# Low parts of weights issued later in the gate-matrix loop, and a pick's gelu and gate moved on ScalarE

## The chip, the core and the metric

The kernel runs on one core of one Trainium2 chip. The core has TensorE (PE, matrix products into PSUM; its weight loads are a row of their own, PEld), VectorE (DVE), ScalarE (ACT), GpSimd (POOL) and the queue of SyncE (SP), from which most DMAs are issued. Each engine works through its own list of instructions in order and waits for the others by semaphores. The metric is the device time of one execution in microseconds (us), the median of several runs.

## What is computed

A transformer-like layer over 512 latent tokens of width 1024: attention and a gating branch, and then a retrieval layer ("PEER"), which is the part that the change touches. Each token picks, for each of 8 heads, 16 out of 16384 experts; an expert is a row `u` and a row `v`, and the token's output is the sum of `gelu(x . u) * gate * v` over its 128 picks.

```python
def peer(h, w_query, sub_keys, u_tab, v_tab):
    ...
    best, pos = lax.top_k(cand, PEER_TOPK)
    eidx = jnp.take_along_axis(cidx, pos, axis=-1)
    gate = jax.nn.softmax(best, axis=-1)
    def one(args):
        xb, ib, gb = args
        act = jax.nn.gelu(jnp.einsum('td,thkd->thk', xb, u_tab[ib]), approximate=False) * gb.astype(xb.dtype)
        return jnp.einsum('thk,thkd->td', act, v_tab[ib])
```

## The kernel before

The 512 tokens are four tiles of 128. Three of them (`NB` = 3, 384 tokens) go the dense way: for each of 128 blocks of 128 experts TensorE computes all products with `u` (a **u pass**, `u_pass`, 24 matmuls into `ps_u`), ScalarE takes the gelu (`gS`), DVE multiplies by a dense matrix of gates (`Gc`, zero where an expert was not picked), and TensorE multiplies by `v` (a **v pass**, `v_pass`, 18 matmuls into `po`). The fourth tile goes by gathers: for each of its 128 picks POOL fetches the rows `u` and `v` (`fetch`, an indirect DMA into `uv`), DVE takes the **dot** with the token (`dot`, a product of 1024 with a running sum, line 846), the gelu and the gate follow, and DVE adds `v` times that to `acc` (`accumulate`, line 855). `gather_step` starts one fetch and takes the dot of the pick fetched three steps ago; `gather_end` finishes the picks in the list `pend`; `gather_to(share)` takes steps until a share of the picks is done.

All products are in three matmuls (`mm3`) of values split into a high and a low part. For each weight tile a DMA on SP's queue loads `w_raw` (four buffers), ScalarE rounds it to the **high part** `w_hi` (line 173), and DVE subtracts to get the **low part** `w_lo` (line 184, function `w_low`). `w_get` asks for the tiles of a pass and starts loads and splits of later ones. `hold[0]` decides when low parts are issued: if it is false, at once behind the high part; if it is true, they wait in `lows` until somebody calls `w_low`.

The dense gates are made in the **gate-matrix loop**, 48 turns (`batches`) of 8 tokens each. A turn i issues, in this order: `one_hots_b` of turn i+1 (8 instructions of DVE, `oh_b`), `gate_matrix` (16 matmuls of TensorE into `ps_G` from `oh_b` and `oh_a`, and two copies of ScalarE to `stg`), one u pass (with its gelu on ScalarE, and with the split of a weight tile for a later one), `one_hots_a` of turn i+2 (8 squares and a Relu of ScalarE, `oh_a`), some 2.8 us of top-16 and merge work for another token tile while there is any (`advance`), `gather_end`, and from turn 10 to turn 41 `gather_to`, 0.8 steps a turn. There are two buffers of `oh_b` and three of `oh_a`.

Behind it comes the **value stage**, 128 turns: a v pass each, from turn 74 on a u pass too up to turn 124, `a_hi` (DVE's `at`, ScalarE's `ah`), `a_lo` (DVE's `al`), and picks at the end of a turn. The lists of PE, DVE, ACT and POOL stand in the order in which this code is written (`manual_schedule`); the order of SP's queue is set by the scheduler.

Of the kernel before, what the change touches and what calls it, by code (L numbers as in the profile page):

```python
# [18 lines left out]
AF = mybir.ActivationFunctionType  # L19
ALU = mybir.AluOpType  # L20
# [38 lines left out]
def body(ctx, nc, tc, a, out):  # L59
# [91 lines left out]
    lows, hold = deque(), [False]  # L151
# [27 lines left out]
    def w_low(upto=None):  # L179

        while lows and (upto is None or lows[0][0] <= upto):
            i, lo, r, hi = lows.popleft()
            eng = nc.gpsimd if order[i] in on_pool else nc.vector
            eng.tensor_tensor(lo, r, hi.bitcast(F32), op=ALU.subtract)  # L184
# [385 lines left out]
    with tc.tile_pool(name="sg1", bufs=1) as s1, tc.tile_pool(name="sg2", bufs=2) as s2:  # L570
# [6 lines left out]
        with tc.tile_pool(name="pz", bufs=1, space=PSUM) as pzp, tc.tile_pool(name="pu", bufs=2, space=PSUM) as pu:  # L577
# [100 lines left out]
            for n in range(8):  # L678
                g = gate(0, n, gs_d)
# [152 lines left out]
    G_FROM = 10  # L832
    steps = [(t, k) for t in range(NB, NT) for k in range(P)]
    n_steps = len(steps)
    coming, pend = [], []

    def fetch(t, k):
        g = ge.tile([P, 2 * D], F32, name="uv", bufs=LEAD + 2)
# [4 lines left out]
    def dot(t, k, g):  # L843
        act = sm.tile([P, 1], F32, name="act")
        junk = ge.tile([P, D], BF16, name="dj")
        nc.vector.scalar_tensor_tensor(junk, g[:, :D], 1.0, h2A[t - NB], op0=ALU.mult, op1=ALU.mult, accum_out=act)  # L846
        return t, k, g, act

    def accumulate(t, k, g, act):
        nc.scalar.activation(act, act, AF.Gelu)  # L850
        nc.vector.tensor_tensor(act, act, gate[:, t, k:k + 1], op=ALU.mult)
        if k == 0:
            nc.vector.tensor_scalar_mul(acc[t - NB], g[:, D:], act)
        else:
            nc.vector.scalar_tensor_tensor(acc[t - NB], g[:, D:], act, acc[t - NB], op0=ALU.mult, op1=ALU.add)  # L855

    def gather_end(left=0):
        while len(pend) > left:
            accumulate(*pend.pop(0))

    def gather_step():
        gather_end(1)
        if len(coming) == LEAD or (coming and not steps):
            pend.append(dot(*coming.pop(0)))
        if steps:
            coming.append(fetch(*steps.pop(0)))

    def gather_to(share):
        while steps and n_steps - len(steps) < n_steps * share:
            gather_step()  # L870

    gS = {}
    with tc.tile_pool(name="k1", bufs=1, side="right") as k1:
# [104 lines left out]
        def advance(us):  # L978

            while us > 0 and any(todo):  # L980
                q = todo[0] or todo[1]
                d = next(q[0], None)
                if d is None:
                    q.popleft()
                else:
                    us -= d
            return any(todo)
# [74 lines left out]
        with tc.tile_pool(name="pg", bufs=3, space=PSUM) as pgp, tc.tile_pool(name="k2", bufs=2, side="right") as k2:  # L1062
            stg = {}

            pks, oas, obs = {}, {}, {}

            def picks_of(t):

                while t not in pks:
                    while t not in done:  # L1070
                        advance(1.0)
                    ef = efs.pop(t)
                    pt = pgp.tile([P, 3, P], F32, name="ps_pk", bufs=1)
                    for k in range(2):
                        nc.tensor.transpose(pt[:, k], ef[:, k].rearrange("p h k -> p (h k)"), ident)
                    nc.tensor.transpose(pt[:, 2], gate[:, t], ident)
                    pks[t] = k2.tile([P, 3, P], F32, name="pk")
                    nc.scalar.activation(pks[t], pt, AF.Copy)
                return pks[t]

            def one_hots_a(t, o):

                pk = picks_of(t)
                oa = oas[t, o] = k2.tile([P, 8, P], F32, name="oh_a", bufs=3)
                for i in range(8):
                    k = o * 8 + i
                    nc.scalar.activation(oa[:, i], iota, AF.Square, scale=-1.0, bias=pk[:, 1, k:k + 1])  # L1087
                nc.scalar.activation(oa, oa, AF.Relu, scale=-1.0, bias=ones[:, 0:1])

            def one_hots_b(t, o):  # L1090

                t0 = o * 8
                pk = picks_of(t)
                ob = obs[t, o] = k2.tile([P, 8, P], F32, name="oh_b")
                for i in range(8):
                    nc.vector.tensor_scalar(ob[:, i], iota, pk[:, 0, t0 + i:t0 + i + 1], pk[:, 2, t0 + i:t0 + i + 1],  # L1096
                                            op0=ALU.is_equal, op1=ALU.mult)

            def gate_matrix(t, o):

                oa, ob = oas.pop((t, o)), obs.pop((t, o))
                if o % 2 == 0:
                    stg[0] = k2.tile([P, NBLK // GCH, 16, GCH], F32, name="stg")
                for q in range(2):
                    pG = pgp.tile([P, 4, P], F32, name="ps_G")
                    for i in range(4):
                        nc.tensor.matmul(pG[:, i], oa[:, q * 4 + i], ob[:, q * 4 + i], start=True, stop=True)  # L1107
                    tt = o % 2 * 8 + q * 4
                    nc.scalar.activation(stg[0][:, :, tt:tt + 4].rearrange("p c t g -> p t c g"),
                                         pG.rearrange("p t (c g) -> p t c g", g=GCH), AF.Copy)  # L1110
                if o % 2:
                    tt = t * P + o // 2 * 16
                    nc.sync.dma_start(G_d[:, :, tt:tt + 16].rearrange("c p t g -> p c (t g)"),
                                      stg[0].rearrange("p c t g -> p c (t g)"))

            batches = [(t, o) for t in range(NB) for o in range(16)]
            while 0 not in done:
                advance(4.0)
                next_u()
            for _ in range(UA):  # L1120
                next_u()
            one_hots_a(*batches[0])
            for _ in range(UB):
                next_u()
            one_hots_a(*batches[1])
            one_hots_b(*batches[0])
            for i, (t, o) in enumerate(batches):
                if i + 1 < len(batches):
                    one_hots_b(*batches[i + 1])
                gate_matrix(t, o)  # L1130
                if nu[0] < n_ahead - RESERVE:
                    next_u()
                if i + 2 < len(batches):
                    one_hots_a(*batches[i + 2])
                advance(2.8)
                gather_end()
                if i >= G_FROM:
                    gather_to(PICKS_G * (i + 1 - G_FROM) / (G_TO - G_FROM) if i < G_TO else 0)
            advance(1000.0)
            while nu[0] < n_ahead:  # L1140
                next_u()


    with tc.tile_pool(name="e1", bufs=2, side="right") as e1, \
# [53 lines left out]
        for b in range(NBLK):  # L1198
            if b == 0:
                gelu_back(0)  # L1200
                gelu_back(1)
                g_load(0)
                parts = a_lo(*a_hi(0))
            if b + 2 < NBLK:
                gelu_back(b + 2)
            u_w = None
            if b >= SPILL and b + AHEAD < NBLK:
                u_w = w_get("u", b + AHEAD)
            else:
                v_w = w_get("v", b)  # L1210
            ah, al = parts
            nxt = None
            if b + 1 < NBLK:
                if (b + 1) % GCH == 0:
                    g_load((b + 1) // GCH)
                nxt = a_hi(b + 1)
            w_low()
            if nxt is not None:
                parts = a_lo(*nxt)
            if u_w is not None:  # L1220
                gS[b + AHEAD] = u_pass(b + AHEAD, u_w)
                v_w = w_get("v", b)
            if b == NBLK // 2:
                nc.sync.dma_start(gg2, rows_d[3:4].to_broadcast([P, D]))
            if b < NBLK - TAIL:
                v_pass(b, *v_w, ah, al, range(NB))
            else:
                tail.append((b, *v_w, ah, al))
            gather_end()
            if b < SPILL:  # L1230
                gather_to(PICKS_G + PICKS_V * (b - 3) / (SPILL - 4))
            else:
                gather_to(PICKS_G + PICKS_V + (1 - PICKS_G - PICKS_V) * (b + 1 - SPILL) / (NBLK - SPILL - 7))
            if not steps and coming:
                gather_step()
            w_low()
            if b == NBLK - 2:
                while coming:
                    gather_step()
                gather_end()  # L1240
                xn = [x_back(t) for t in range(NT)]
                for t in range(NB, NT):
                    finish(t, acc[t - NB], xn[t])
# [79 lines left out]
```

## Time and profile before

| | us |
|---|---|
| median of 3 runs | 2053.46 (2052.76 to 2057.22) |
| the profiled execution, its own time | 2056.82 |
| its span, from first to last instruction | 2055.1 |
| busy PE, DVE, ACT, POOL | 1934.7 (94%), 1610.0 (78%), 1007.2 (49%), 387.9 (19%) |

Times of day in the rows are us from the span's start. The rows of the trace give start, length, engine, line and what was written from what; a bracket at the end of a row holds the idle time of the engine before it and what ended that. A granted clock of 1.00 is TensorE's upper level (2.4 GHz), 0.50 its lower (1.2 GHz). The gate-matrix loop lies between 945 and 1270 us, the value stage from 1289 us on. An instruction's row is longer than the time after which its engine starts the next one, since they overlap at their ends.

### The profile page before, as it was taken

The numbers are of one execution on the slowest core, as the hardware profiler recorded it, in microseconds if no ns is written. First come the engines' busy times: TensorE is split into PE (matmuls) and PEld (weight loads), VectorE is DVE, ScalarE is ACT, GpSimd is POOL, SyncE is SP. The second block draws the span as 40 slices with busy tenths as digits, with TensorE's granted clock in tenths as the row PEclk, the third lists the DMA queues.
The fourth block names the chain that finished last, engine by engine and source line by source line (L and its number), as shares of the span: only waits on it lengthen the run. The fifth ranks groups of instructions, "written<-read, shape, count | busy, mean of one in ns | idle before, by whom it ended". The sixth has DMA issues, their size and how long they took to land.

```text
span 2055.1 us, 28329 instructions
## 1 busy us (share of the span) xinstructions
PE 1934.7 (94%) x10042; PEld 1697.7 (83%) x10042; DVE 1610.0 (78%) x3108; ACT 1007.2 (49%) x1947; POOL 387.9 (19%) x237
## 2 busy tenths in 40 slices
PE   6889999999999899888899999999999999999997
PEld 5767888887878798788889999788888899998996
DVE  7667777747755657999998785688888799898887
ACT  4335555535433355447888987333333333333333
POOL 0023232101000124330001110011111233333321
PEclk9999999999989999999999999999999999999999
DMA  8843323256755354445569998889899799989982
GB/s 320 281 159 91 89 82 96 84 193 217 236 166 199 128 160 151 135 169 203 179 194 322 309 324 284 301 315 338 326 335 321 269 343 356 341 322 340 346 314 96
DMA packets 171229, 484.40 MB, mean 236 GB/s; under 512 B 14384, under 2 KB 82896, under 8 KB 152528
## 3 DMA queue, kind: packets, MB, share of 16 engines
q1 hardware_dynamic: 152656, 348.37, 50.6%
q0 software_dynamic: 18432, 134.23, 17.9%
q8 instruction: 79, 1.29, 0.2%
q14 instruction: 62, 0.51, 0.1%
HBM read 424.72 MB, written 49.43 MB: 231 GB/s over the span
## 4 chain that ended last, share of the span: by engine, by line
PE 64%; DVE 15%; issue 6%; ACT 4%; DMA 2%; POOL 1%; SPq 0%; ACTq 0%; POOLq 0%; DVEq 0%
PE po L202 8%; PE po L203 8%; PE po L204 8%; PE ps_u L204 5%; PE ps_u L203 5%; PE ps_u L202 5%; PE ps_G L1107 2%; DVE w_lo L184 2%; PE ps_proj L202 2%; PE ps_proj L203 2%; PE ps_proj L204 2%; PE ps_s L488 2%; PE ps_o L522 2%; ACT oh_a L1087 1%; DVE oh_b L1096 1%
## 5 line engine op out<-in xcount | busy, mean ns | idle before, releaser
L173 ACT ACTIVATE w_hi<-w_raw 128x1024 fp32r<-128x1024 f32 x370 | 391.0, 1057 | 469.2 <-issue 263.3
L184 DVE TENSOR_TENSOR w_lo<-w_raw,w_hi 128x1024 fp32r<-128x1024 f32 x330 | 404.9, 1228 | 150.8 <-ACT w_hi L173 150.4
L839 POOL DMA_INDIRECT uv<-in_uv,eidx x128 | 208.7, 1631 | 876.9 <-DVE acc L855 537.5
L204 PE MATMUL ps_u<-h2B,w_lo 128*128 128x384 f32 x1024 | 348.3, 340 | 16.4 <-DVE w_lo L184 16.4
L202 PE MATMUL ps_u<-h2B,w_hi 128*128 128x384 f32 x1024 | 352.2, 344 | 1.1 <-ACT h2B L771 1.1
L203 PE MATMUL ps_u<-h2B,w_hi 128*128 128x384 f32 x1024 | 347.0, 339 | 0.6 <-DVE r L84 0.6
L202 PE MATMUL po<-w_hi,ah 128*128 128x512 f32 x768 | 304.5, 396 | 7.8 <-ACT ah L1180 7.8
L203 PE MATMUL po<-w_lo,ah 128*128 128x512 f32 x768 | 304.3, 396 | 0.9 <-DVE w_lo L184 0.9
L204 PE MATMUL po<-w_hi,al 128*128 128x512 f32 x768 | 304.2, 396 | 0.0
L204 PEld LDWEIGHTS ps_u<-h2B,w_lo 128*128 128x128 f32 x1024 | 194.3, 190 | 19.3 <-DVE w_lo L184 19.3
L202 PEld LDWEIGHTS ps_u<-h2B,w_hi 128*128 128x128 f32 x1024 | 194.9, 190 | 4.1 <-ACT h2B L771 1.4
L203 PEld LDWEIGHTS ps_u<-h2B,w_hi 128*128 128x128 f32 x1024 | 194.6, 190 | 3.8 <-DVE r L84 1.0
L202 PEld LDWEIGHTS po<-w_hi,ah 128*128 128x128 f32 x768 | 144.7, 188 | 41.0 <-ACT ah L1180 8.1
L204 PEld LDWEIGHTS po<-w_hi,al 128*128 128x128 f32 x768 | 144.7, 188 | 35.1
L203 PEld LDWEIGHTS po<-w_lo,ah 128*128 128x128 f32 x768 | 144.7, 188 | 34.1 <-DVE w_lo L184 1.3
L855 DVE SCALAR_TENSOR_TENSOR acc<-uv,act,acc 128x1024 f32<-128x1024 f32 x127 | 163.2, 1285 | 4.5
L846 DVE SCALAR_TENSOR_TENSOR dj<-uv,h2A 128x1024 bf16<-128x1024 f32 x128 | 156.2, 1220 | 0.9
L184 POOL TENSOR_TENSOR w_lo<-w_raw,w_hi 128x1024 fp32r<-128x1024 f32 x40 | 98.0, 2452 | 248.2 <-ACT w_hi L173 245.1
L1178 DVE TENSOR_TENSOR at<-gS,Gc 128x384 f32<-128x384 f32 x128 | 121.1, 946 | 9.1 <-DMA gS<-gS_d 9.0
L1180 ACT ACTIVATE ah<-at 128x384 fp32r<-128x384 f32 x128 | 66.2, 518 | 122.1 <-DVE at L1178 121.8
L813 ACT ACTIVATE gS<-ps_u 128x384 f32<-128x384 f32 x128 | 62.8, 491 | 128.7 <-PE ps_u L204 128.3
L1107 PE MATMUL ps_G<-oh_b,oh_a 128*128 128x128 f32 x768 | 100.7, 284 | 24.8 <-DVE oh_b L1096 24.3
(308 smaller groups left out, 3503.3 us busy)
## 6 DMA issues: line engine op xcount, KB each, us to landing
w_raw<-in_uT SPq DMA_DIRECT2D x128, 512.0 KB, 5.6
w_raw<-in_uv SPq DMA_DIRECT2D x128, 512.0 KB, 6.3
w_raw<-in_w SPq DMA_DIRECT2D x120, 512.0 KB, 3.8
G_d<-stg SPq DMA_DIRECT2D x24, 1024.0 KB, 5.8
Gc<-G_d SPq DMA_DIRECT2D x16, 1536.0 KB, 10.1
ada_w<-in_wada SPq DMA_DIRECT2D x32, 512.0 KB, 10.0
w_raw<-in_wada SPq DMA_DIRECT2D x32, 512.0 KB, 4.3
gS_d<-gS SPq DMA_DIRECT2D x74, 192.0 KB, 4.0
```

Source lines behind the costliest of these rows:

```text
L173: nc.scalar.activation(hi, r, AF.Copy)
L184: eng.tensor_tensor(lo, r, hi.bitcast(F32), op=ALU.subtract)
L202: nc.tensor.matmul(ps, lh, rh, start=first, stop=False)
L203: nc.tensor.matmul(ps, lh, rl, start=False, stop=False)
L204: nc.tensor.matmul(ps, ll, rh, start=False, stop=last)
L813: nc.scalar.activation(g, ps, AF.Gelu)
L839: nc.gpsimd.indirect_dma_start(out=g, out_offset=None, in_=a["uv"], in_offset=bass.IndirectOffsetOnAxis(ap=eidx[:, t - NB, k:k + 1], axis=0))
L846: nc.vector.scalar_tensor_tensor(junk, g[:, :D], 1.0, h2A[t - NB], op0=ALU.mult, op1=ALU.mult, accum_out=act)
L855: nc.vector.scalar_tensor_tensor(acc[t - NB], g[:, D:], act, acc[t - NB], op0=ALU.mult, op1=ALU.add)
L1107: nc.tensor.matmul(pG[:, i], oa[:, q * 4 + i], ob[:, q * 4 + i], start=True, stop=True)
L1178: nc.vector.tensor_tensor(at, gS.pop(b), Gc[b // GCH][:, :, b % GCH], op=ALU.mult)
L1180: nc.scalar.activation(ah, at, AF.Copy)
```

## The change

Three things. In the gate-matrix loop `hold[0]` is true, and `w_low` is called at the end of each turn, behind the picks. A pick's gelu is in a function of its own, `gelus`, called in the gate-matrix loop just ahead of `advance` and in the value stage behind `w_get`, ahead of `a_hi`; picks whose dot is done wait for it in the list `dots_`. And the multiplication by the pick's gate, an instruction of DVE on 128x1, is an activation of ScalarE (Copy with a scale) behind the gelu.

```diff
-    coming, pend = [], []
+    coming, dots_, pend = [], [], []
...
+    def gelus():
+
+        while dots_:
+            t, k, g, act = dots_.pop(0)
+            nc.scalar.activation(act, act, AF.Gelu)
+            nc.scalar.activation(act, act, AF.Copy, scale=gate[:, t, k:k + 1])
+            pend.append((t, k, g, act))
+
     def accumulate(t, k, g, act):
-        nc.scalar.activation(act, act, AF.Gelu)
-        nc.vector.tensor_tensor(act, act, gate[:, t, k:k + 1], op=ALU.mult)
         if k == 0:
...
-    def gather_end(left=0):
-        while len(pend) > left:
+    def gather_end():
+        gelus()
+        while pend:
             accumulate(*pend.pop(0))
 
     def gather_step():
-        gather_end(1)
+        if len(dots_) + len(pend) > 1:
+            gather_end()
         if len(coming) == LEAD or (coming and not steps):
-            pend.append(dot(*coming.pop(0)))
+            dots_.append(dot(*coming.pop(0)))
...
             one_hots_b(*batches[0])
+            hold[0] = True
             for i, (t, o) in enumerate(batches):
...
+                gelus()
                 advance(2.8)
                 gather_end()
                 if i >= G_FROM:
                     gather_to(PICKS_G * (i + 1 - G_FROM) / (G_TO - G_FROM) if i < G_TO else 0)
+                w_low()
...
             ah, al = parts
+            gelus()
             nxt = None
```

DVE's list in a turn of the gate-matrix loop with a pick, from one `one_hots_b` to the next; `acc` is the accumulate, `dj` the dot. Before:

```order
L1096 TENSOR_SCALAR oh_b<-iota,pk 128x128 x8
L184 TENSOR_TENSOR w_lo<-w_raw,w_hi 128x1024
L851 TENSOR_TENSOR act<-act,gate 128x1
L855 SCALAR_TENSOR_TENSOR acc_5712<-uv,act,acc_5712 128x1024
L846 SCALAR_TENSOR_TENSOR dj,act<-uv,h2A_5331 128x1024
L1096 TENSOR_SCALAR oh_b<-iota,pk 128x128 x8
```

and after the change:

```order
L1104 TENSOR_SCALAR oh_b<-iota,pk 128x128 x8
L861 SCALAR_TENSOR_TENSOR acc_5712<-uv,act,acc_5712 128x1024
L846 SCALAR_TENSOR_TENSOR dj,act<-uv,h2A_5331 128x1024
L184 TENSOR_TENSOR w_lo<-w_raw,w_hi 128x1024
L1104 TENSOR_SCALAR oh_b<-iota,pk 128x128 x8
```

The low part has moved from the place ahead of the accumulate to the place behind the dot, and the multiply is gone.

ScalarE's list in a turn of the same loop, from the gelu of one pick to that of the next, after the change:

```order
L854 ACTIVATE act<-act,gate 128x1
L1117 ACTIVATE stg<-ps_G 128x4x16x8 x2
L173 ACTIVATE w_hi<-w_raw 128x1024
L813 ACTIVATE gS<-ps_u 128x384
L1095 ACTIVATE oh_a<-iota,pk 128x128 x8
L1096 ACTIVATE oh_a<-oh_a,ones 128x1024
L853 ACTIVATE act<-act 128x1
```

Before, the pick's gelu (there line 850) stood at the same place, behind the Relu of `oh_a`; new is the gate behind it.

ScalarE's list in the value stage, in turns with a u pass. Before:

```order
L1180 ACTIVATE ah<-at 128x384
L813 ACTIVATE gS<-ps_u 128x384
L173 ACTIVATE w_hi<-w_raw 128x1024
L850 ACTIVATE act<-act 128x1
L173 ACTIVATE w_hi<-w_raw 128x1024
```

and after the change:

```order
L1191 ACTIVATE ah<-at 128x384
L813 ACTIVATE gS<-ps_u 128x384
L173 ACTIVATE w_hi<-w_raw 128x1024 x2
L853 ACTIVATE act<-act 128x1
L854 ACTIVATE act<-act,gate 128x1
```

The gelu has moved behind the second high part, next to `ah` of the following turn, and the gate is behind it.

## Rows read from the trace of the kernel before

**Rows 1.** Busy time: stretch, length, PE, PEld, DVE, ACT, POOL (instructions), clock, DMA share, GB/s.

```profile
1055.00:1256.00 201.00, 186.71 (x1212) 183.12 (x1213) 160.78 (x374) 178.34 (x414) 33.38 (x23) 0.99 0.92 304
...
1300.00:2030.00 730.00, 729.06 (x3438) 627.84 (x3437) 637.51 (x841) 269.40 (x453) 170.36 (x100) 1.00 0.88 319
```

**Rows 2.** Who waited for whom, 1300 to 2030 us: total, times, longest.

```profile
PE po L203 <- DVE w_lo L184: 0.9, 1, 0.9
```

**Rows 3.** Who waited for whom, 1055 to 1256 us: total, times, longest.

```profile
DVE act L851 <- ACT act L850: 27.6, 17, 3.2
...
PE ps_G L1107 <- DVE oh_b L1096: 15.7, 12, 2.0
DVE w_lo L184 <- ACT w_hi L173: 10.9, 6, 2.7
```

**Rows 4.** TensorE's gate matmuls in order of time, 1076 to 1112 us: start, length.

```profile
1077.01 2.20 PE L1107 MATMUL ps_G<-oh_b,oh_a 128*128 128x128 f32 x16 [1.24 <-DVE oh_b L1096]
...
1083.22 1.95 PE L1107 MATMUL ps_G<-oh_b,oh_a 128*128 128x128 f32 x16
...
1090.59 2.19 PE L1107 MATMUL ps_G<-oh_b,oh_a 128*128 128x128 f32 x16 [1.24 <-DVE oh_b L1096]
...
1096.80 1.95 PE L1107 MATMUL ps_G<-oh_b,oh_a 128*128 128x128 f32 x16
...
1102.76 1.95 PE L1107 MATMUL ps_G<-oh_b,oh_a 128*128 128x128 f32 x16
...
1110.12 2.08 PE L1107 MATMUL ps_G<-oh_b,oh_a 128*128 128x128 f32 x15 [1.23 <-DVE oh_b L1096]
```

**Rows 5.** ScalarE and DVE in one turn, in order of time, 1083 to 1091 us.

```profile
1083.42 0.49 ACT L813 ACTIVATE gS<-ps_u 128x384 f32<-128x384 f32 x1 [1.60 <-PE ps_u L204]
...
1084.53 1.22 DVE L184 TENSOR_TENSOR w_lo<-w_raw,w_hi 128x1024 fp32r<-128x1024 f32 x1
...
1086.28 1.15 ACT L1088 ACTIVATE oh_a<-oh_a,ones 128x1024 f32<-128x1024 f32 x1
1087.34 0.18 ACT L850 ACTIVATE act<-act 128x1 f32<-128x1 f32 x1
1087.43 1.07 ACT L1109 ACTIVATE stg<-ps_G 128x512 f32<-128x512 f32 x2
1087.56 0.16 DVE L851 TENSOR_TENSOR act<-act,gate 128x1 f32<-128x1 f32 x1 [1.81 <-ACT act L850]
1087.75 1.28 DVE L855 SCALAR_TENSOR_TENSOR acc<-uv,act,acc 128x1024 f32<-128x1024 f32 x1
...
1090.10 1.11 DVE L1096 TENSOR_SCALAR oh_b<-iota,pk 128x128 f32<-128x128 f32 x4
```

**Rows 6.** The chain that ended last, 940 to 1290 us: start, length, engine, line.

```profile
1013.21 1.13 DVE w_lo L184
```

**Rows 7.** TensorE in order of time at four places, three with a wait before.

```profile
894.35 0.45 PE L204 MATMUL ps_u<-h2B,w_lo 128*128 128x384 f32 x1 [2.22 <-DVE w_lo L184]
...
909.10 0.45 PE L204 MATMUL ps_u<-h2B,w_lo 128*128 128x384 f32 x1 [2.11 <-DVE w_lo L184]
...
1055.66 3.17 PE L1107 MATMUL ps_G<-oh_b,oh_a 128*128 128x128 f32 x16 [2.04 <-DVE oh_b L1096]
...
1063.35 2.29 PE L1107 MATMUL ps_G<-oh_b,oh_a 128*128 128x128 f32 x16
```

**Rows 8.** Busy time and clock in the 4 us after those waits, as in rows 1.

```profile
894.00:898.00 4.00, 3.65 (x21) 3.65 (x22) 3.79 (x22) 0.00 (x0) 0.00 (x0) 1.00 0.46 131
909.00:913.00 4.00, 3.90 (x13) 3.90 (x14) 3.90 (x13) 0.42 (x1) 3.84 (x2) 0.58 0.69 229
1056.00:1060.00 4.00, 4.00 (x21) 4.00 (x20) 3.97 (x9) 3.54 (x8) 0.00 (x0) 0.57 0.17 18
```

**Rows 9.** DVE in the loop's first turn, in order of time.

```profile
955.91 1.22 DVE L184 TENSOR_TENSOR w_lo<-w_raw,w_hi 128x1024 fp32r<-128x1024 f32 x1 [1.41 <-ACT w_hi L173]
```

**Rows 10.** DMA issues of the page: count, KB each, us to landing.

```profile
w_raw<-in_uT SPq DMA_DIRECT2D x128, 512.0 KB, 5.6
```

## The prediction

> **What bounds the kernel now.** I read the busy time by stage first [rows 1], then TensorE's own waits in the one stage where it is not full, then who releases them. From 1300 to 2030 us, the stage of the value passes, TensorE is busy for 729.06 of 730 us at a granted clock of 1.00: that stage runs at the rate of its matmuls, and what DVE or ScalarE saves there is worth at most the 0.9 us that TensorE waited for a low part [rows 2]. From 1055 to 1256 us, the turns of the gate-matrix loop that also take picks, TensorE is busy for 186.71 of 201 us while DVE and ScalarE are busy for 160.78 and 178.34. From 945 to 1055 us DVE has the top-16 and merge work of another tile in the same turns.
>
> In the pick turns TensorE waits for one thing, DVE's `oh_b`: 15.7 us in 12 waits, the longest 2.0 [rows 3]. Without that one it is 13.7 us in eleven waits of 1.24. The starts of the gate matmuls [rows 4] show the pattern: steps of 6.21, 7.37, 6.21, 5.96 and 7.36 us, 33.11 us for five turns, with a wait of 1.24 before 1077.01, 1090.59 and 1110.12. A turn without a wait takes 5.96.
>
> One turn shows why [rows 5]. The u pass of a turn ends and ScalarE starts its gelu at 1083.42; then come eight `oh_a`, the Relu at 1086.28 and the pick's gelu at 1087.34. DVE has done the low part long before (1084.53 to 1085.75) and idles 1.81 us for that gelu; then multiply, accumulate, dot, and at 1090.10 the first `oh_b`, which the gate matmul at 1090.59 needs [rows 4]. From 1083.42 that is 7.17 us. TensorE's next turn of matmuls, begun at 1083.22, is over at 1089.35, and it stands for 1.24. So ScalarE's gelu, and after it everything that DVE queues before `oh_b`, is the path that sets the end here; **the low part is not on it**, since it lies in DVE's wait.
>
> **The change part by part.** *The low part moves behind accumulate and dot.* In the new order DVE has `oh_b`, accumulate, dot, low part, `oh_b`. ScalarE's queue still has the pick's gelu behind the Relu: in this loop `gelus()` stands where the gelu stood. So DVE reaches the accumulate earlier and only waits longer (1.81 becomes about 3.0), and the low part now stands between the gelu and `oh_b`. Its price is not the 1.22 of its row but the 1.13 after which DVE begins the next instruction [rows 6]. Queued behind it is `oh_b`, and for that waits the next gate matmul. Each of the eleven waits grows from 1.24 to 2.37: 11 x 1.13 = **+12.4 us**. A turn with an accumulate and no dot has 1.2 us less in its chain and still makes no wait, and a turn with a dot alone waits for no gelu; these two of five turns stay as they are.
>
> *The gate on ScalarE.* DVE loses the multiply, 0.19 us from 1087.56 to 1087.75 [rows 5]. ScalarE gains an instruction of the same shape as the gelu (0.18) in the same chain, since the accumulate now waits for it. I take 0.0 per wait, by those two rows; the bounds are -0.1 (it overlaps the gelu's end, as the next instruction starts 0.09 after the gelu) and +0.2 (it starts only when the gelu's result is written), so -1 to +2 us over eleven. The Trainium skill, "ScalarE: Activation LUTs", section "Rules for kernel authors", speaks against the move: a multiply belongs on VectorE, and about 0.3 us are to be counted for an ACTIVATE. By that figure each wait would grow by 0.12 more and the sum by 1.3 us; the trace has 0.18 for this shape [rows 5].
>
> *The longer wait and the clock.* What a wait of 2.4 us does to TensorE's clock no row shows; the nearest are three waits of about 2 us. Before 1055.66 it waited 2.04 [rows 7], and the granted clock was 0.57 over the next 4 us [rows 8], mostly the lower level of 1.2 GHz; the gate matmuls took 3.17 instead of 2.19, and the next turn began 7.69 us later instead of 6.21, so it cost 1.48. After 2.11 us at 909.10 the clock was 0.58. After 2.22 us at 894.35 it stayed at 1.00. The eleven waits of 1.24 never lowered it: the whole stretch has 0.99 [rows 1], and the one drop, 4 x 0.43 = 1.7 us of clock in 201, makes that up. With 2.37 the new waits are longer than all three. I take the share of these three, two in three: 11 x 2/3 x 1.48 = **+10.9 us**; the bounds are none (0) and all (16.3). The Trainium skill, "TensorE: Matmul & The Clock Gate", section "HAM oscillation", describes a loop that falls to the lower clock in every round because its bursts of matmuls are shorter than the waits between them, and has loops with long bursts stay at the upper one. By that this loop, with 12 to 19 us of matmuls between waits, would stay up, and the sum would be without the 10.9; the drop at 1055.66 [rows 7, 8] disagrees.
>
> *The first turns.* In the turns before picks DVE fills its time with merge work, and the low part costs it the same at either place. One wait goes: DVE stood 1.41 us for the high part at 955.91 [rows 9], and will have merge work there. **-1.4 us.**
>
> *SP's queue.* Loads of weights wait for the low part that frees their buffer. They now issue some 4 us later, and the scheduler puts several behind the next spill `gS_d`. A load is issued about three turns (some 20 us) before the high part reads it, and lands after 5.6 us [rows 10]: I cost this at nothing; it would cost if loads came two turns later. POOL's gathers wait for the accumulate, which keeps its place or comes earlier, and three picks lie ahead. Nothing.
>
> *The value passes.* There gelu and gate now go ahead of `ah` on ScalarE, a turn after the dot, and the accumulate waits for nothing. DVE gets time that nobody waits for. The two instructions delay `ah` by under 0.6 us, and its reader, the next v pass, is over 4 us away. At most the 0.9 us of TensorE's wait go [rows 2]. **-0.9 us.** TensorE is next, at 729 of 730.
>
> The sum is 12.4 + 10.9 - 1.4 - 0.9 = **+21.0 us**. On the profiled execution's 2056.82 us that is 2077.8; that execution lies 3.4 us over the median of the three runs, and on the median, 2053.46, it is 2074.5.
>
> **The rivals.** *The clock stays up.* The waits grow, no drop follows: 12.4 - 2.3 = +10.1, 2063.6 us. For it: 894.35, and a whole loop so far without one from a wait of 1.24. Against: the other two of the three.
>
> *Every wait drops it*, and the copy costs its 0.2: 12.4 + 16.3 + 2.2 - 1.4 - 0.9 = +28.6, 2082.1 us. For it: 2.37 is longer than any of the three; against: 894.35.
>
> *Faster.* The low part waited 10.9 us for ScalarE's high part in six of the pick turns [rows 3]. If those waits ended later than the pick's gelu, it is the low part that holds `oh_b` back today, and with it behind the dot the eleven waits go: -13.7 - 2.3 = -16.0, 2037.5 us. This decides if the low part ends after the gelu's end. Against: it ends 1.6 us before the gelu starts [rows 5], and DVE waits 27.6 us in 17 turns for the gelu itself [rows 3].
>
> *No change.* The longer chain finds cover, because ScalarE comes to the gelu earlier when TensorE stands (its Relu and copies are then done sooner): only the 2.3 us of the small gains are left, 2051 to 2053. Against: the chain begins at the u pass's end, so ScalarE cannot start it early.
>
> **How the numbers follow.** The forecast has 0.60, the clock staying up 0.14, every wait dropping it 0.14, no change 0.06, faster 0.06. The first three are slower: 0.88. A difference of 0.2% (4 us) is about what a measurement of this kernel can tell from no change. The range goes from the rival with no drop, with the copy's -1, at 2062, to the one with all of them and no small gains, at 2085; it leaves out the two cases of 0.06.
>
> **What would show it.** Right: DVE's waits for the gate copy longer than the old ones for the gelu, in the same turns; eleven waits of TensorE for `oh_b` near 2.4 us, with five turns taking some 35.4 us and more; a granted clock near 0.94 in these turns (1.7 us lost in each of seven drops, in some 220 us); gate matmuls of about 3 us after some waits; the value passes as long as before. Wrong: waits of 1.2 as before (the low part found cover), waits gone (it was the hindrance), or a value stage in which TensorE stands, for loads that came late or for `ah`.

## The result, and the profile after

The changed kernel takes **2075.24 us** (median of 4 runs, 2074.33 to 2078.71) against 2053.25 (2052.76 to 2057.22) of the kernel before in the same runs: a ratio of **1.0105, with a 95% interval from 1.0093 to 1.0118**. The forecast was 2074.5, in a range from 2062 to 2085; for the profiled execution it was 2077.8. The profiled execution of after took 2078.71 us (span 2076.9) and has a mean clock of 0.976; that of before took 2056.82 (span 2055.1).

The view of busy time by stretch, with the columns of [rows 1]; the pick turns are now 223 us long, and the value stage begins later:

```profile
1055.00:1278.00 223.00, 195.07 (x1194) 190.91 (x1194) 153.35 (x341) 182.07 (x429) 38.57 (x23) 0.94 0.83 275
1322.00:2052.00 730.00, 730.00 (x3444) 628.96 (x3443) 624.05 (x737) 297.52 (x558) 172.62 (x100) 1.00 0.88 319
```

TensorE, which was busy for 186.71 of 201 us in the pick turns, now stands for 28 of 223, at a granted clock of 0.94 instead of 0.99. In the value stage it no longer stands at all: the 0.9 us of [rows 2] are gone. That this is the change's doing isn't shown: in low_only below, whose value stage is that of before, TensorE doesn't stand there either. The loss lies in the pick turns. Who waited for whom there (total, times, longest), to be put beside [rows 3]:

```profile
DVE acc L861 <- ACT act L854: 65.9, 22, 7.7
...
PE ps_G L1115 <- DVE oh_b L1104: 27.9, 12, 2.5
...
DVE w_lo L184 <- ACT w_hi L173: 3.7, 1, 3.7
```

DVE's wait for the pick's activations has gone from 27.6 to 65.9 us: it reaches the accumulate earlier, since the low part is no longer ahead of it, and waits. Its waits for high parts, 10.9 us, are nearly gone, and none of that is a gain, because those were waits inside the longer wait. TensorE's waits for `oh_b` have grown from 15.7 to 27.9. TensorE's gate matmuls in order of time show where (start, length, and in the bracket the wait before):

```profile
1075.49 3.29 PE L1115 MATMUL ps_G<-oh_b,oh_a 128*128 128x128 f32 x16 [2.50 <-DVE oh_b L1104]
...
1083.15 1.95 PE L1115 MATMUL ps_G<-oh_b,oh_a 128*128 128x128 f32 x16
...
1091.78 1.54 PE L1115 MATMUL ps_G<-oh_b,oh_a 128*128 128x128 f32 x10 [2.50 <-DVE oh_b L1104]
...
1152.41 2.19 PE L1115 MATMUL ps_G<-oh_b,oh_a 128*128 128x128 f32 x16 [2.50 <-DVE oh_b L1104]
...
1158.62 2.19 PE L1115 MATMUL ps_G<-oh_b,oh_a 128*128 128x128 f32 x16
```

The first three rows are turns of [rows 4] (the third ends with the view, after ten of its sixteen matmuls), and a wait of 2.50 stands where 1.24 stood. The turn that begins at 1075.49 takes 7.66 us until the next one's gate matmuls; the one at 1152.41, after a wait of the same length, takes 6.21. The clock makes the difference (the same view, 4 us behind each wait, as in [rows 8]):

```profile
1076.00:1080.00 4.00, 4.00 (x20) 4.00 (x19) 3.40 (x7) 3.31 (x7) 0.70 (x1) 0.57 1.02 301
...
1153.00:1157.00 4.00, 4.00 (x28) 3.98 (x28) 3.40 (x7) 3.48 (x7) 0.79 (x1) 1.00 0.98 271
```

One turn of ScalarE and DVE, which answers to [rows 5]:

```profile
1083.35 0.49 ACT L813 ACTIVATE gS<-ps_u 128x384 f32<-128x384 f32 x1 [2.98 <-PE ps_u L204]
...
1086.21 1.15 ACT L1096 ACTIVATE oh_a<-oh_a,ones 128x1024 f32<-128x1024 f32 x1
1087.27 0.18 ACT L853 ACTIVATE act<-act 128x1 f32<-128x1 f32 x1
1087.48 0.29 ACT L854 ACTIVATE act<-act,gate 128x1 f32<-128x1 f32 x1
...
1087.81 1.28 DVE L861 SCALAR_TENSOR_TENSOR acc<-uv,act,acc 128x1024 f32<-128x1024 f32 x1 [4.45 <-ACT act L854]
...
1089.01 1.22 DVE L846 SCALAR_TENSOR_TENSOR dj<-uv,h2A 128x1024 bf16<-128x1024 f32 x1
...
1090.16 1.22 DVE L184 TENSOR_TENSOR w_lo<-w_raw,w_hi 128x1024 fp32r<-128x1024 f32 x1
1091.29 0.85 DVE L1104 TENSOR_SCALAR oh_b<-iota,pk 128x128 f32<-128x128 f32 x3
```

From the u pass's end at 1083.35 to the first `oh_b` at 1091.29 there are now 7.94 us where there were 6.68. The low part takes 1.13 of the additional 1.26 (1090.16 to 1091.29). The rest, 0.13, is the gate: from the start of the gelu to the start of the accumulate it is 0.54 us here (1087.27 to 1087.81) and was 0.41 in before (1087.34 to 1087.75), with DVE's multiply in it. Loads of weights land as before:

```profile
w_raw<-in_uT SPq DMA_DIRECT2D x128, 512.0 KB, 5.4
```

The whole account, from the two profiled executions: the loop begins 1.0 us earlier; its turns 0 to 15 are 1.5 shorter (104.86 to 103.37); **turns 15 to 47 are 25.1 longer** (211.37 to 236.43, between the starts of their gate matmuls); the way to the first v pass is 0.4 longer, and the value stage 1.2 shorter. That makes +21.8, the difference of the two spans. The 25.1 are 13.1 of longer waits (26.8 for 13.6), 11.4 of eight turns at a lower clock, and 0.7 of three turns like the one at 1158.62, whose gate matmuls take 2.19 instead of 1.95 with no wait before them; 0.3 go off, because the clock fell behind the wait before turn 15 in before and not here.

Two of the small parts aren't tied to the change. Over the twelve kernels the loop begins anywhere from 948.1 to 953.7 us. And from the first v pass to the end of the span, where before takes 765.8 and after 764.6, low_only and the three kernels with additions (all below), which have the value stage of before, take 764.0 to 764.2.

### The profile page after: what moved, and what is told of

It reads as the page before. It is cut to its first block, busy times and chain, and to the rows that moved or that the text cites. A ratio compares the mean times of both kernels' runs of the same rounds, so it can differ in the third digit from the quotient of the medians.

```text
span 2076.9 us, 28251 instructions
## 1 busy us (share of the span) xinstructions
PE 1941.9 (94%) x10042; PEld 1706.7 (82%) x10042; DVE 1590.0 (77%) x2980; ACT 1042.5 (50%) x2075; POOL 397.0 (19%) x237
## 4 chain that ended last, share of the span: by engine, by line
PE 61%; DVE 16%; issue 7%; ACT 5%; DMA 4%; POOL 1%; SPq 0%; DVEq 0%; ACTq 0%; POOLq 0%
PE po L202 8%; PE po L203 8%; PE po L204 8%; PE ps_u L204 5%; PE ps_u L203 5%; PE ps_u L202 5%; DVE w_lo L184 3%; DMA w_raw<-in_wada 3%; PE ps_G L1115 2%; PE ps_proj L202 2%; PE ps_proj L203 2%; PE ps_proj L204 2%; PE ps_s L488 2%; ACT oh_a L1095 2%; PE ps_o L522 2%
## 5 line engine op out<-in xcount | busy, mean ns | idle before, releaser
L839 POOL DMA_INDIRECT uv<-in_uv,eidx x128 | 217.2, 1697 | 886.7 <-DVE acc L861 738.7
L861 DVE SCALAR_TENSOR_TENSOR acc<-uv,act,acc 128x1024 f32<-128x1024 f32 x127 | 162.6, 1280 | 66.8 <-ACT act L854 65.9
L1115 PE MATMUL ps_G<-oh_b,oh_a 128*128 128x128 f32 x768 | 107.7, 297 | 38.2 <-DVE oh_b L1104 37.7
L1115 PEld LDWEIGHTS ps_G<-oh_b,oh_a 128*128 128x128 f32 x768 | 101.8, 204 | 45.8 <-issue 33.2
```

Source lines behind the costliest of these rows:

```text
L839: nc.gpsimd.indirect_dma_start(out=g, out_offset=None, in_=a["uv"], in_offset=bass.IndirectOffsetOnAxis(ap=eidx[:, t - NB, k:k + 1], axis=0))
```

## The experiments

My theory: in the pick turns the path goes from the u pass's end over ScalarE's `oh_a`, Relu, gelu and then DVE's accumulate and dot to `oh_b`; what stands behind the gelu counts in full and what stands ahead of it on DVE counts nothing; and the longer wait lowers TensorE's clock in some turns. Rivals: the gate on ScalarE is what costs; or the low part costs by being DVE's work at all, wherever it stands; or the clock fell for another reason than the length of the wait. The stretch from turn 15 to turn 47 is the measure beside the time (starts of the gate matmuls in each kernel's trace):

| kernel | median us | ratio to before, 95% | turns 15 to 47, us | eleven waits, us |
|---|---|---|---|---|
| before | 2053.25 | | 211.37 | 13.6 |
| after | 2075.24 | 1.0105 (1.0093 to 1.0118) | 236.43 | 26.8 |
| gate_only | 2057.32 | 1.0003 (0.9993 to 1.0012) | 212.64 | 13.8 |
| low_only | 2073.9 | 1.0088 (1.0071 to 1.0105) | 232.68 | 26.1 |
| low_mid | 2054.09 | 0.9994 (0.9984 to 1.0003) | 212.64 | 13.8 |
| dot_first | 2045.04 | 0.996 (0.9944 to 0.9975) | 202.39 | 1.4 |
| gelu_early | 2036.58 | 0.9904 (0.9887 to 0.992) | 196.59 | none |
| early_mul | 2036.04 | 0.9905 (0.9889 to 0.9922) | 193.24 | none |
| early_mul_low0 | 2037.19 | 0.9906 (0.989 to 0.9923) | 193.56 | none |

Each ratio is against runs of the kernel before that were made beside it, whose medians differ by a microsecond or two from the one in the first line.

### The two parts apart

**gate_only** is after without the moved low part:

```diff
-            hold[0] = True
...
-                w_low()
```

> The changed kernel with the low parts issued as before (at once behind the high part), so that only the gelu's place and the gate on ScalarE are left of the change. Theory (the low part's place costs nearly all): the eleven waits of TensorE are 1.24 + 0.13 = 1.37 us, no drops of the clock beyond the one at turn 15, +1.4 us for the copies, -0.9 in the value stage: 2053 to 2055 us. Rival (the accumulate's wait for two activations, or the value stage's new order, is what costs): 2065 us or more, waits near 2.4 us in the same turns.

Measured: 2057.32 us, no difference from before that can be told (the runs of before beside it have 2055.28), and 2.3 over the range that I had given. Where before has two waits of 1.24 one after the other, it has one of 1.37 and one of 1.11; TensorE's waits from 1063 to 1290 us (total, times, longest):

```profile
PE ps_G L1115 <- DVE oh_b L1104: 13.8, 11, 1.4
```

The stretch of turns 15 to 47 is 1.3 us longer, eleven times 0.12. Only a part of it shows as a wait: ahead of a wait of 1.11 the gate matmuls of the turn before take 2.19 us instead of 1.95, while DVE is still writing their `oh_b`. So the copy does cost its tenth of a microsecond, and it is not what made after slow.

**low_only** is before with the low part at the end of a turn, gelu and multiply as they were:

```diff
             one_hots_b(*batches[0])
+            hold[0] = True
...
                     gather_to(PICKS_G * (i + 1 - G_FROM) / (G_TO - G_FROM) if i < G_TO else 0)
+                w_low()
```

> The kernel before with the low parts alone moved to the end of the turn; gelu and gate as before. Theory: eleven waits of 1.24 + 1.13 = 2.37 us, about seven or eight drops of the clock, 2072 to 2076 us. Rival (gate on ScalarE or the new order in the value stage): 2052 to 2056.

Measured: 2073.9 us, in the expected range. TensorE's waits in the same stretch, and the busy time by stretch (columns as in [rows 1]):

```profile
PE ps_G L1107 <- DVE oh_b L1096: 26.1, 11, 2.4
```

```profile
1063.00:1245.00 182.00, 158.28 (x984) 155.19 (x983) 130.07 (x302) 147.47 (x338) 33.54 (x20) 0.95 0.85 282
```

The waits are 2.37 in all eleven turns, to the hundredth what the row of 1.13 in [rows 6] made of 1.24 (one has 2.40). The clock falls behind six of the eleven, where I had expected seven or eight. 12.4 of waits and six slow turns at about 1.5 are 21.4; turns 15 to 47 are 21.3 longer. This part alone makes 21.3 of the 25.1 that after loses there; the rest is the copy and two more drops of the clock.

### The same work at another place

**low_mid** is after with the low part ahead of the accumulate, still held back to the end of the u pass:

```diff
                 advance(2.8)
+                w_low()
                 gather_end()
...
-                w_low()
```

> The changed kernel with the call that issues the low parts moved from behind the dot to just ahead of the accumulate, that is into DVE's wait for the gelu, but still behind the merge work. Theory (what counts is whether the low part lies behind the gelu, not that it is late in the turn): waits of 1.37 as in gate_only, and the gain of 1.4 us in the first turns is kept: 2051 to 2054 us. Rival (holding low parts back at all, with the loads on SP's queue that then issue later, costs): 2060 or more, waits for high or low parts in the trace.

Measured: 2054.09 us, the time of before and within a tenth of the expected range. DVE and TensorE in order of time:

```profile
1074.18 2.19 PE L1115 MATMUL ps_G<-oh_b,oh_a 128*128 128x128 f32 x16 [1.36 <-DVE oh_b L1104]
...
1075.75 1.22 DVE L184 TENSOR_TENSOR w_lo<-w_raw,w_hi 128x1024 fp32r<-128x1024 f32 x1
...
1077.24 0.29 ACT L854 ACTIVATE act<-act,gate 128x1 f32<-128x1 f32 x1
...
1077.57 1.29 DVE L861 SCALAR_TENSOR_TENSOR acc<-uv,act,acc 128x1024 f32<-128x1024 f32 x1 [0.61 <-ACT act L854]
```

The low part ends at 1076.97, DVE waits 0.61 more for the gate, and TensorE's waits are those of gate_only. DVE has done the same instructions as in after: the same 1.22 us cost 21 us of time behind the gelu and nothing ahead of it. The gain in turns 0 to 15 is kept (103.34 us). With this the rival that the low part costs wherever it stands falls.

**gelu_early** is after with the pick's gelu and gate at the start of the next turn, ahead of the gate matrix's copies and the u pass's gelu on ScalarE:

```diff
+                gelus()
                 gate_matrix(t, o)
...
-                gelus()
                 advance(2.8)
```

> The changed kernel with the pick's gelu and gate moved on ScalarE from behind the Relu of oh_a to the start of the turn, ahead of the copies to stg; the low part stays at the end of the turn. Theory (the gelu's place in ScalarE's list is the head of the chain): accumulate, dot and low part no longer wait for the u pass, the eleven waits go, 13.6 us below the kernel before and 0.9 to 2.5 more: 2037 to 2040 us. Rival (DVE's own length of a turn, or ScalarE's, is the bound): waits of about 1 us or more stay, 2050 or more.

Measured: **2036.58 us**, 1% faster than before and 0.4 below the expected range. TensorE's gate matmuls, busy time by stretch, and the waits of DVE and of TensorE's weight load in that stretch:

```profile
1083.06 1.95 PE L1115 MATMUL ps_G<-oh_b,oh_a 128*128 128x128 f32 x16
...
1089.02 1.95 PE L1115 MATMUL ps_G<-oh_b,oh_a 128*128 128x128 f32 x16
```

```profile
1063.00:1245.00 182.00, 181.95 (x1200) 177.63 (x1199) 149.23 (x336) 180.31 (x432) 32.48 (x22) 1.00 0.99 338
```

```profile
DVE acc L861 <- ACT act L854: 14.5, 20, 1.6
PEld ps_G L1115 <- ACT oh_a L1096: 4.3, 15, 0.4
```

All eleven waits are gone, with the low part still at the end of the turn. That settles the path: it was the gelu that came late, and everything on DVE behind it hung on that. The next thing that shows is ScalarE, busy for 180.31 of 182 us: in fifteen turns TensorE's weight load waits up to 0.4 for `oh_a`, and most of these turns take 6.23 us instead of 5.97.

**dot_first** leaves the gelu where it is in after and puts low part and dot ahead of the accumulate, into DVE's wait:

```diff
                 advance(2.8)
-                gather_end()
+                w_low()
                 if i >= G_FROM:
                     gather_to(PICKS_G * (i + 1 - G_FROM) / (G_TO - G_FROM) if i < G_TO else 0)
-                w_low()
+                while pend:
+                    accumulate(*pend.pop(0))
```

> The changed kernel with the low part and then the dot ahead of the accumulate in each turn, so that both lie in DVE's wait for the gelu and only the accumulate stands between gelu and oh_b. Theory: the chain is 7.17 + 0.13 - 1.2 = 6.1 us, against 5.93 that TensorE has work for: waits of 0.1 to 0.2 in place of 1.24, about 12 us below the kernel before and 1 to 2 more in the first turns and the value stage: 2038 to 2042 us. Rival (DVE does not have the time, or the gathers' buffers come free too late): 2050 or more.

Measured: 2045.04 us, faster than before by 0.4%, but three microseconds over what I had expected. Six waits of 0.22 to 0.26 are left of the eleven; in order of time:

```profile
1102.39 0.18 ACT L853 ACTIVATE act<-act 128x1 f32<-128x1 f32 x1
...
1102.93 1.28 DVE L861 SCALAR_TENSOR_TENSOR acc<-uv,act,acc 128x1024 f32<-128x1024 f32 x1 [2.36 <-ACT act L854]
...
1104.14 1.34 DVE L1104 TENSOR_SCALAR oh_b<-iota,pk 128x128 f32<-128x128 f32 x4
...
1104.62 0.57 PE L1115 MATMUL ps_G<-oh_b,oh_a 128*128 128x128 f32 x3 [0.22 <-DVE oh_b L1104]
```

The accumulate still lies between gelu and `oh_b`, and for that I had expected a chain of 6.1 us a turn and waits of 0.1 to 0.2. What I had missed is that a turn gets longer where no wait is seen: most turns take 6.2 to 6.4 us, not 5.97, and in most of them the sixteen gate matmuls take 2.2 to 2.3 us instead of 1.95, because DVE is still writing `oh_b` while they run.

### The length of the wait and the clock

Three kernels are before with one thing more: an addition on DVE whose result nobody reads, behind each dot in the loop, of 440 elements, of 1024, and twice 1024.

```diff
             pend.append(dot(*coming.pop(0)))
+            if filler[0]:
+                for n in filler[0]:
+                    pad = ge.tile([P, D], BF16, name="dj")
+                    nc.vector.tensor_tensor(pad[:, :n], h2A[0][:, :n], h2A[0][:, :n], op=ALU.add)
```

> The kernel before with an addition of 128x440 on VectorE behind each dot of the gate-matrix loop, about 0.5 us that nobody needs. Theory (DVE's time between gelu and oh_b goes to TensorE's wait one for one): waits of 1.24 + 0.5 = 1.74 in the eleven places, +5.5 us, and the clock: no drop was seen after waits of up to 1.6 us here, drops after 1.8 to 1.9 elsewhere, so none to three, 2058 to 2063 us. Rival (some of DVE's time is hidden): under 2056.

> The same with 128x1024, as long as a low part (1.13 us). Theory: as low_only, waits of 2.37 in the eleven places and six to nine drops of the clock, 2073 to 2078 us (no gain in the first turns). Rival (it is the low part as such, its wait for the high part or the load that waits for it): under 2068.

> The same with two of them (2.26 us). Theory: waits of about 3.5 us in the eleven places, +25 us, and a drop of the clock after each, about 1.45 each, +16: 2092 to 2097 us. Rival (drops do not depend on the wait's length and stay at eight of eleven): 2088 to 2091.

Measured, one run each: 2064.59, 2080.92 and 2102.02 us. All three lie over what I had expected, by 1.6, 2.9 and 5.0 microseconds, and further from the rivals' times. I had left out that the addition also stands in turns 10 to 14: from turn 0 to turn 15 these kernels take 0.7, 1.3 and 2.6 us more than before, most of it in the wait before turn 15, which is 2.69, 3.29 and 4.55 instead of 2.04. A part of the rest may be the comparison of one run with a median: against the profiled execution of before, their spans are longer by 7.7, 24.0 and 45.1 us, where the expectations, put against the median, amounted to 5 to 10, 20 to 25 and 39 to 44. TensorE's waits for `oh_b` from 1063 to 1290 us with half an addition and with one, then the busy time by stretch with half, one and two:

```profile
PE ps_G L1112 <- DVE oh_b L1101: 19.1, 11, 1.9
```

```profile
PE ps_G L1112 <- DVE oh_b L1101: 25.4, 11, 2.5
```

```profile
1063.00:1245.00 182.00, 164.76 (x1058) 160.06 (x1057) 151.60 (x347) 155.90 (x362) 30.68 (x21) 0.99 0.92 301
```

```profile
1063.00:1245.00 182.00, 159.22 (x975) 155.06 (x973) 151.61 (x317) 144.18 (x332) 29.25 (x20) 0.94 0.86 277
```

```profile
1063.00:1245.00 182.00, 152.45 (x904) 148.19 (x903) 159.69 (x307) 135.03 (x310) 26.29 (x18) 0.92 0.80 254
```

The kernel with one addition has nine waits of 2.5 us, as in after, two of 1.5, and the clock of 0.94, and no part of the change: its low part is where it was. So what after pays for is some 1.2 us of DVE's work at this place, whatever the work. Counted over the traces, the waits before the eleven turns and the turns behind them that took about 1.4 us longer at a lower granted clock:

| waits before these turns, us | kernels | waits | clock fell behind |
|---|---|---|---|
| 1.1 to 1.4 | before, gate_only, low_mid | 33 | 0 |
| 1.46 to 1.92 | half an addition, and two turns of one | 13 | 1 |
| 2.24 to 2.54 | low_only, after, one addition | 31 | 21 |
| 2.92 to 3.79 | two additions | 11 | 11 |

The wait of 2.03 to 2.06 before turn 15, which is not among the eleven, is followed by a fall in four of the nine kernels that have it. So in this loop how often the clock falls goes with the length of the wait, and since one addition brings the falls without any part of the change, they need nothing of the change but the wait. The length is not all of it, though. Outside the loop, behind a wait of 1.80 us near 202 us, the clock falls in eleven of the twelve kernels. And which of the waits of 2.4 us are followed by a drop stays open: the turns are not the same ones in low_only, in after and with one addition (turn 28 drops in the first alone, turn 18 in the other two alone), and none of these runs varied anything that would tell it.

### A version that beats both

**early_mul** is gelu_early with the multiplication by the gate back on DVE, to give ScalarE room:

```diff
             nc.scalar.activation(act, act, AF.Gelu)
-            nc.scalar.activation(act, act, AF.Copy, scale=gate[:, t, k:k + 1])
...
     def accumulate(t, k, g, act):
+        nc.vector.tensor_tensor(act, act, gate[:, t, k:k + 1], op=ALU.mult)
```

> As gelu_early (low part at the end of a turn, the pick's gelu at the start of a turn), with the gate's multiplication on DVE as in the kernel before. Theory: with the eleven waits gone ScalarE sets the pace of the later turns (180 of 182 us busy, turns of 6.23 us instead of 5.96 in some fifteen of them), so taking its extra activation of some 0.3 us away brings these turns back to near 5.97: 15 x 0.26 = 3.9 us, 2032.5 to 2035 us, no turn of TensorE waits for oh_b, ScalarE's busy time in the same stretch falls by about 4 to 5 us. Rival: the 6.23 comes from something else (DMA, the DVE chain), and the time stays at 2036.5; a multiply of 0.19 us on DVE costs nothing by either, since DVE waits 14.5 us for the gate copy there.

Measured: 2036.04 us, the same as gelu_early; the expected 2032.5 to 2035 was missed. The step itself did what was expected: the turns are back at 5.97, and turns 15 to 47 are 3.35 us shorter (196.59 to 193.24). The gain is not in the time: each of the two ratios is known to about 3.4 us either way, so 3.35 us can be lost in that. In the profiled execution the loop began 2.1 us later than in that of gelu_early, in code that the two have in common, and at the loop's end 1.0 us turned into a longer wait for the first `ah` (7.84 for 6.82). The chain that ended last, there, in order of time:

```profile
1250.45 1.24 DVE w_lo L184
1251.70 5.61 DMA w_raw<-in_uv
...
1257.60 1.06 ACT w_hi L173
1258.69 1.24 DVE w_lo L184
1259.94 0.33 SPq L160
1260.32 0.48 SPq L822
1260.84 6.74 DMA gS<-gS_d
1267.60 0.86 DVE at L1189
1268.61 0.53 ACT ah L1191
1269.18 0.79 PE po L202
```

Between the last u pass and the first v pass it is transfers that end last: a weight load that waits for the buffer of a low part, and behind it in SP's queue the first gelus that come back from memory. That an earlier end of the loop is paid back there isn't shown: from turn 47 to the first v pass the twelve kernels take 21.3 to 22.7 us, in no order with the loop's end.

**early_mul_low0** is early_mul without the held low part, so that all that is left of the change is `gelus` as a function, at the gelu's new place in the loop and at that of after in the value stage:

```diff
-            hold[0] = True
...
-                w_low()
             advance(1000.0)
```

> As early_mul, with the low part issued at once behind its high part again, as in the kernel before; all that is left of the changes is the pick's gelu at the start of a turn. Theory: the low part then waits in DVE's list for ScalarE's high part ahead of accumulate and dot, but the accumulate has no long wait of its own any more, so that there is little to lie in; the high part comes early in a turn (some 0.2 us after the gate matmuls begin), so the low part still ends some 2 us ahead of accumulate and dot's end and TensorE waits for no oh_b: same as early_mul within 2 us, plus the 1.4 us of the first turns, 2033 to 2037 us. Rival: the place at the end is what keeps DVE from waiting, and with the low part ahead TensorE waits some tenths for oh_b in the eleven turns: 2038 to 2042.

Measured: 2037.19 us, 1.2 over early_mul and 0.2 over the expected bound, with turns 15 to 47 as long (193.56) and 1.8 us more from turn 0 to turn 17. With the gelu early, DVE has room in every turn, and it no longer matters at which end of it the low part stands. The gain of 1% is the gelu's place alone: of some 17 us, 17.8 lie in turns 15 to 47 (211.37 to 193.56).

## Why the prediction was right, step by step

The mechanism came as forecast, and so did most of the terms. That the sum came so near (+21.0, and +21.8 between the profiled executions) is in part luck: the loop's two terms were forecast at 23.3 and its pick turns lost 25.1, and 1.0 of the difference went into a start that was earlier for no reason that the change gives.

*The path.* That ScalarE's gelu and what DVE has behind it set the end [rows 5], and that the low part lay in DVE's wait, held: low_mid shows the second, gelu_early the first.

*The low part, +12.4.* low_only has eleven waits of 2.37, the forecast number. In after the waits sum to 26.8 for 13.65 of before, +13.1: the 0.7 above the forecast belong to the next term, and so do the 0.7 of the three turns with slower gate matmuls.

*The gate on ScalarE, 0.0.* This term was sized wrong, within its bounds. I took the copy to be like the gelu, 0.18, because the shape is the same; its row has 0.29, and the chain grew by 0.13 each time with DVE's multiply taken out of it. gate_only has it by itself, +1.3 us over the stretch. The figure of the Trainium skill, "ScalarE: Activation LUTs", section "Rules for kernel authors", is about 0.3 us for an ACTIVATE with a pointer operand, and agrees with the 0.29 of the copy, whose scale is one; the gelu of 0.18 has none in its call. The +1.3 us that the prediction worked out from that figure, and set aside for the gelu's row, is what gate_only has. The scale operand should have kept me from taking the gelu's row for the copy.

*The clock, +10.9.* In after the clock fell behind eight of the eleven waits, and those turns took 1.4 us longer, together 11.4. Over the three kernels with such waits it is 21 of 31, the two in three that three rows gave by luck as much as by weight. The trace of before had two more waits between 2 and 2.7 us: behind 2.02 at 835.71 the clock stayed, behind 2.63 at 845.22 it was 0.63 over 4 us. With them the share is three in five. "TensorE: Matmul & The Clock Gate" of the Trainium skill, section "HAM oscillation", by which this loop would stay up, is contradicted by these 21. One thing in the step was wrong though its number was right. I priced a drop by the turn at 1055.66 [rows 7], 7.69 for 6.21 us. At that place a drop costs little: of nine kernels with that wait of 2.03 to 2.06, four show it, and before, with the drop, takes 13.98 us from turn 15 to turn 17, after, without it, 13.70, because there the next turn waits 1.14 instead. The price held because in the pick turns behind it nothing takes a slow turn back.

*The first turns, -1.4.* -1.5 from turn 0 to turn 15, and low_mid has the same.

*SP's queue, nothing; the value passes, -0.9.* Loads landed in 5.4 us, and no turn of the loop waits for one. The value stage took 1.2 us less, its wait among it, but kernels with the value stage of before took as little, so this term is not shown to be the change's.

*The rivals.* "The clock stays up" failed by the eight turns, "every wait drops it" by the three that kept it. "No change" failed as it said itself: ScalarE cannot begin its chain before the u pass ends. "Faster" named the low part as what holds `oh_b` back, and low_mid shows that it does not. A gain of about the size that it gave was there all the same (2036.6 for 2037.5), by the place of the gelu, which the change left where it was in this loop.

## What to carry to other kernels

What an instruction costs in an engine's list depends on which side of that engine's longest wait it stands: ahead of the wait 1.22 us of DVE were free, behind it they cost 1.13 in each of the eleven turns that had waited before, and nearly as much again in clock. Before moving work out of a queue's way, find the instruction that the next wait of the bounding engine hangs on and ask if the source of that chain can come earlier; here a tiny activation ahead of the u pass's gelu instead of behind it was worth 1%. And where a change makes TensorE's waits longer, price the turns behind the waits as well as the waits.

## What the runs showed of the hardware that was not expected

- A copy of 128x1 with a scale operand takes 0.29 us on ScalarE where a gelu of that shape takes 0.18, and begins 0.21 after the gelu's start.
- In this loop the share of waits behind which the clock falls rises with their length, from none of 33 (1.1 to 1.4 us) over 21 of 31 (2.24 to 2.54) to all of 11 (2.92 to 3.79); a slow turn costs about 1.4 us where nothing covers it, and 0.3 or less where the next turn would have waited anyway. Outside it, near 202 us, a wait of 1.80 is followed by a fall in eleven of twelve kernels.
- Sixteen gate matmuls take 1.95 us when `oh_b` is there, and 2.2 to 2.3 when DVE writes it while they run: a turn can lose 0.3 us to another engine's pace with no wait in its rows.
